# Building one-hot coefficient tables: second-key compares in bf16, cast to fp32 by ScalarE

## The chip, the core and the metric

The kernel runs on one core of a Trainium2 chip. The metric is the device time in microseconds of one execution, the median of several. The work is in fp32, with bf16 used for values that are exact in it (small whole numbers, zeros and ones).

## What is computed

One layer of a diffusion backbone over 128 context tokens and 512 latent tokens, width 1024: a projection, retention and neighbourhood attention, an output projection, and then a PEER layer, which is what matters here. Cut to that:

```python
def peer(x, wq, keys, u, v):          # 8 heads, product keys, 128 * 128 experts, top 16 per head
    q = (xb @ wq).reshape(TOKEN_BLOCK, PEER_HEADS, PEER_DKEY)
    s1 = jnp.einsum('nhd,hkd->nhk', q[..., :half], keys[:, 0])
    s2 = jnp.einsum('nhd,hkd->nhk', q[..., half:], keys[:, 1])
    ...
    eidx = jnp.take_along_axis(cidx, sel, axis=-1)        # i1 * 128 + i2
    gate = jax.nn.softmax(top, axis=-1)
    act = jax.nn.gelu(jnp.einsum('nd,nhkd->nhk', xb, u[eidx]))
    return jnp.einsum('nhk,nhkd->nd', gate * act, v[eidx])
```

Each of the 640 tokens picks 128 experts; for each, a row of `u` is dotted with the token, and a row of `v` is added with the weight `gate * act`.

## The kernel before, in words

Tokens go in five blocks of 128: block 0 is the context, blocks 1 to 4 the latents.

**The `u` half.** For all five blocks the rows of `u` are fetched by indirect DMA, issued by GpSimd: one gather brings one row to each of 128 tokens (512 KB), 128 gathers per block, 640 in all. They land in a handful of buffers in the arena. VectorE takes each with one dot product (`scalar_tensor_tensor` over 128x1024 with an accumulator, `gathers`, L1438, L1488), which frees the buffer for the next gather. The finding of the experts (`topk`, L1349) is VectorE work as well, with some casts on ScalarE.

**The `v` half.** For block 4 it is done in the same way, with 128 more gathers. Blocks 0 to 3 do without gathers: the weights of 128 tokens are written out as a dense coefficient table of 128 x 128 experts per token, and all of `v` (64 MB) is streamed through TensorE against it. `Dense.product(0)` does blocks 0 and 1, `Dense.product(1)` blocks 2 and 3; each has 512 matmuls 128x512, four for each tile of `v` (two blocks by two halves). `v` is read by SyncE's queue into a ring of six buffers.

**The tables.** `Dense.build(b)` (L1571) makes the table of block b, `W[b % 2]`. Its start turns the expert numbers into two key tables (`keys[:, 0]` the first key, `keys[:, 1]` the second, in bf16, one column per token) and the weights into `cT`; there is one set of these (`tabs`), so one build follows the other. Then it goes over the 128 tokens in pairs. For a pair, VectorE compares the first keys with 0..127 into `eq` (bf16) and the second keys into `B_` (fp32); ScalarE multiplies `eq` with the weight of each token into `A_` (fp32), two instructions; TensorE multiplies `B_` with `A_`, one matmul 128x128 per token, into a PSUM bank. After two pairs ScalarE copies the bank of four tokens into the table. I call two pairs, with that copy, a group: 32 groups per build, 128 in all. `eq`, `A_` and `B_` have two buffers each. For blocks 0 and 1 the copy writes with a stride (the table lies expert by token), for blocks 2 and 3 it writes whole rows, into rows that `product(0)` has done with. So `build(0)` and `build(1)` come before `product(0)`, `build(2)` runs beside it, and `build(3)` lies round its end, before `product(1)` can use its second table. `build(0)` runs beside `key_scores` (L913), the last stage of the projections.

**The order.** Nothing is issued as it is written. `Plan` records every operation (L167), gives it a cost from its engine, size and types (`cost`, L192), and a list scheduler (`forward`, L293, `backward`, `order`, L223) sets the order on each engine; line L365 of the trace, where the order is emitted, is therefore the line of nearly all instructions. On an engine, instructions run in that order, and one that waits holds up all behind it.

Of the kernel before, what the change touches and what calls it, by code (L numbers as in the profile page):

```python
# [12 lines left out]
BF16 = mybir.dt.bfloat16  # L13
# [3 lines left out]
AF = mybir.ActivationFunctionType  # L17
OP = mybir.AluOpType
# [3 lines left out]
P = 128  # L22
# [346 lines left out]
def layer(ctx: ExitStack, tc: tile.TileContext, a: dict):  # L369
    nc = Plan(tc.nc)  # L370
# [9 lines left out]
    iota2 = st.tile([P, P, 2], BF16, name="iota2")  # L380
# [32 lines left out]
    def bank():  # L413
        return ps.alloc([512], lo=banks[0], hi=banks[1])
# [11 lines left out]
    def mm(out, lhsT, rhs, start, stop):  # L426
        nc.tensor.matmul(out, lhsT=lhsT, rhs=rhs, start=start, stop=stop)
        k, m = lhsT.shape[0], int(np.prod(lhsT.shape[1:]))
        n = int(np.prod(rhs.shape[1:]))
        up = lambda v: 32 if v <= 32 else 64 if v <= 64 else 128  # L430
        clk["PE"] += 4 * n / 2400.0 * up(k) / 128 * up(m) / 128

    def tr(out, in_):
        nc.tensor.transpose(out, in_, ident)
        clk["PE"] += 0.216
# [118 lines left out]
    oneh, eqs, tabs, scb, spare = [], [], [], [], []  # L554

    def reserve():

        all_ = ar.alloc([19, P], lo=0, hi=12 * 256 // UNIT).ap
        oneh[:] = [all_[:, 4 * i:4 * i + 4].rearrange("s (z n) i -> s z n i", z=2) for i in range(2)]
        eqs[:] = [all_[:, 8 + i].bitcast(BF16).rearrange("s (i n) -> s i n", n=2) for i in range(2)]  # L560
        tabs[:] = [all_[:, 12], all_[:, 13], all_[:, 14].bitcast(BF16).rearrange("s (z n) -> s z n", z=2)]
        scb[:] = [all_[:, 15:19]]
        spare[:] = [all_[:, 0:8].rearrange("s a b -> s (a b)")]
# [388 lines left out]
    def ctx_front():  # L952
# [123 lines left out]
        ada(2, 1)  # L1076
        make_gates(0, ("g2",))
        reserve()
        done.add("ctx")

# [484 lines left out]
    class Dense:  # L1565
# [5 lines left out]
        def build(self, b):  # L1571

            g, q = divmod(b, 2)
            if self.W[q] is None:
                self.W[q] = ar.alloc([P, P], top=True)
            Wn = self.W[q].ap
            if g == 0:
                Wn = Wn.rearrange("j i n -> j n i")
            while (b, 3) not in cready:
                yield "wait"  # L1580

            bt = bank()
            tr(bt.ap[:, 0:P], cw[b].rearrange("q h k -> q (h k)"))
            cT, ti, keys = tabs
            tii = ti.bitcast(I32)
            id_ = idx[b].rearrange("q h k -> q (h k)")
            for z, (op, s) in enumerate(((OP.arith_shift_right, 7), (OP.bitwise_and, 127))):
                nc.vector.tensor_single_scalar(tii, id_, s, op=op)
                nc.vector.tensor_scalar(ti, tii, 1.0, None, op0=OP.mult)
                tr(bt.ap[:, P * (z + 1):P * (z + 2)], ti)  # L1590
            nc.scalar.copy(cT, bt.ap[:, 0:P])
            nc.scalar.copy(keys, bt.ap[:, P:3 * P].rearrange("s (z n) -> s z n", z=2))
            ps.free(bt)
            full = None
            for m in range(P // 2):
                n0 = 2 * m
                while g == 1 and self.at < min(n0 + 4, P) and n0 % 4 == 0:
                    yield "at"
                eq, A_, B_ = eqs[m % 2], oneh[m % 2][:, 0], oneh[m % 2][:, 1]
                nc.vector.tensor_tensor(eq, iota2, keys[:, 0, None, n0:n0 + 2].to_broadcast([P, P, 2]), op=OP.is_equal)  # L1600
                nc.vector.tensor_tensor(B_, iota2.rearrange("s i n -> s n i"),
                                        keys[:, 1, n0:n0 + 2, None].to_broadcast([P, 2, P]), op=OP.is_equal)
                if n0 % 4 == 0:
                    bw = bank()
                for k in range(2):
                    nc.scalar.activation(A_[:, k], eq[:, :, k], AF.Copy, scale=cT[:, n0 + k:n0 + k + 1])
                if full is not None:
                    nc.scalar.copy(*full)
                    ps.free(last)
                    full = None  # L1610
                for k in range(2):
                    z = n0 % 4 + k
                    mm(bw.ap[:, P * z:P * z + P], B_[:, k], A_[:, k], True, True)
                if n0 % 4:
                    full, last = (Wn[:, n0 - 2:n0 + 2, :], bw.ap.rearrange("j (n i) -> j n i", n=4)), bw
                    yield
            nc.scalar.copy(*full)
            ps.free(last)
# [194 lines left out]
```

## Time and profile before

| | |
|---|---|
| median of three runs | 1906.23 us (1904.07 to 1906.36) |
| profiled execution | 1904.95 us, of which the span from first to last instruction is 1903.1 us |
| busy: PE | 1777.2 us (93%) |
| busy: DVE | 1467.7 us (77%) |
| busy: ACT | 532.2 us (28%) |
| busy: POOL | 834.4 us (44%) |
| mean granted TensorE clock | 0.958 |
| DMA | 658.22 MB, mean 346 GB/s |

PE is TensorE, PEld its loading of weights, DVE VectorE, ACT ScalarE, POOL GpSimd, SP SyncE. Shares are means over stages that have different limits. A record of a matmul 128x512 in fp32 comes twice per matmul. Records of instructions on one engine overlap at their ends, so that what one instruction costs its engine is read from start to start, not from its length.

### The profile page before, as it was taken

Reading aid. Unit: us, or ns where it says so; the run is one execution under the profiler, and the core shown is the slowest. Engines: PE = TensorE matmul, PEld = TensorE weight load, DVE = VectorE, ACT = ScalarE, POOL = GpSimd, SP = SyncE. Lnnn points to the kernel's source line nnn. Section 1 sums busy time; section 2 is a strip of 40 time slices with the busy share of each in tenths; the row PEclk is TensorE's granted clock in tenths of the full one; section 3 lists DMA queues with packets and bytes.
Section 4 is the critical chain, followed back from the end, with each engine's and each line's share of the span. In section 5 each row is a group of like instructions: output and inputs, shape, how many; then the busy total and the mean of one; then the engine's idle time right before and its main releaser. Section 6 shows DMA issues by size and latency. Waiting matters only on the chain.

```text
span 1903.1 us, 21175 instructions
## 1 busy us (share of the span) xinstructions
PE 1777.2 (93%) x6096; PEld 1063.2 (56%) x6096; DVE 1467.7 (77%) x3785; ACT 532.2 (28%) x1368; POOL 834.4 (44%) x779
## 2 busy tenths in 40 slices
PE   7999999999999889867999999899987999999997
PEld 2438454455965466555444444355665666666665
DVE  2246998786879999999999996777998566666666
ACT  1225320133434334698211110122674000000000
POOL 0000467542137666524555544444435344444442
PEclk9998999999979889977999999899997999999999
DMA  9997889988759999857999999999978999999998
GB/s 363 316 327 246 313 278 339 393 311 307 271 178 344 365 336 378 317 177 210 364 408 401 392 408 409 387 409 406 358 242 275 410 409 409 409 409 409 409 409 330
DMA packets 203693, 658.22 MB, mean 346 GB/s; under 512 B 22572, under 2 KB 25900, under 8 KB 203448
## 3 DMA queue, kind: packets, MB, share of 16 engines
q0 software_dynamic: 110592, 402.70, 56.7%
q1 hardware_dynamic: 92984, 254.16, 35.5%
q8 instruction: 49, 0.80, 0.2%
q14 instruction: 68, 0.56, 0.1%
HBM read 645.51 MB, written 11.27 MB: 345 GB/s over the span
## 4 chain that ended last, share of the span: by engine, by line
DMA 27%; DVE 18%; PE 12%; issue 6%; ACT 2%; POOL 1%; DVEq 0%; POOLq 0%; ACTq 0%
DMA arena<-in_u,idx 15%; PE psum L365 12%; DMA arena<-in_v,idx 12%; DVE arena L365 12%; ACT arena L365 2%; DVE psum L365 1%; POOL arena L365 1%; DVE i L365 1%; DVE oh L365 1%; DVE vi L365 1%; DVE cand L365 0%; DVE idx L365 0%; DVE pi L365 0%; DMA w<-xres 0%; DMA out_y<-w 0%
## 5 line engine op out<-in xcount | busy, mean ns | idle before, releaser
L365 PE MATMUL psum<-w,arena 128*128 128x512 f32 (+1 forms) x2548 | 1094.2, 600 | 17.4 <-DVE arena L365 6.5
L365 POOL DMA_INDIRECT arena<-in_u,idx x640 | 711.6, 1112 | 899.8 <-DVE arena L365 486.6
L365 PEld LDWEIGHTS psum<-w,arena 128*128 128x128 f32 (+1 forms) x2548 | 560.4, 229 | 456.3 <-issue 280.2
L365 PE MATMUL psum<-arena 128*128 128x128 f32 (+5 forms) x2532 | 543.4, 366 | 65.3 <-ACT arena L365 34.1
L365 PEld LDWEIGHTS psum<-arena 128*128 128x128 f32 (+2 forms) x2532 | 374.3, 206 | 273.8 <-issue 137.3
L365 DVE SCALAR_TENSOR_TENSOR arena<-arena 128x1024 f32<-128x1024 f32 (+5 forms) x451 | 488.7, 1091 | 27.6 <-DMA arena<-in_u,idx 25.0
L365 DVE SCALAR_TENSOR_TENSOR arena<-arena,psum 128x1024 f32<-128x1024 f32 x256 | 308.4, 1214 | 92.6 <-DMA arena<-in_u,idx 92.6
L365 ACT ACTIVATE arena<-arena 128x128 f32<-128x128 bf16 (+7 forms) x626 | 237.7, 433 | 224.4 <-PE psum L365 103.8
L365 ACT COPY arena<-psum 128x512 f32<-128x512 f32 (+3 forms) x360 | 204.0, 581 | 316.6 <-PE psum L365 287.0
L365 DVE SCALAR_TENSOR_TENSOR psum<-arena,cw,psum 128x1024 f32<-128x1024 f32 x127 | 163.7, 1289 | 96.1 <-DMA arena<-in_v,idx 96.0
L365 DVE TENSOR_TENSOR arena<-iota,arena 128x256 f32<-128x256 bf16 (+1 forms) x512 | 160.7, 355 | 36.1 <-PE psum L365 33.3
L365 POOL DMA_INDIRECT arena<-in_v,idx x128 | 119.9, 937 | 141.5 <-DVE psum L365 118.1
L365 PE MATMUL psum<-arena,w 128*128 128x128 f32 (+1 forms) x640 | 132.0, 365 | 1.6 <-ACT arena L365 1.6
L365 PEld LDWEIGHTS psum<-arena,w 128*128 128x128 f32 x640 | 92.9, 196 | 31.4 <-ACT arena L365 2.3
L365 PE MATMUL psum<-ident,arena 128*128 128x128 f32 x372 | 64.9, 302 | 30.6 <-DVE arena L365 28.1
L365 PEld LDWEIGHTS psum<-ident,arena 128*128 128x128 f32 x372 | 48.7, 157 | 66.2 <-DVE arena L365 32.4
L365 DVE TENSOR_TENSOR arena<-arena 128x256 f32<-128x256 f32 (+6 forms) x131 | 61.0, 497 | 6.6 <-ACT arena L365 3.7
L365 ACT ACTIVATE zz<-dots 128x64 f32<-128x64 f32 x10 | 2.6, 255 | 196.3 <-DVE arena L365 196.3
L365 DVE TENSOR_TENSOR arena<-psum,arena 128x512 f32<-128x512 f32 (+1 forms) x40 | 27.1, 688 | 35.8 <-PE psum L365 34.7
L365 DVE TENSOR_REDUCE arena<-arena 128x8 f32<-128x512 f32 (+1 forms) x17 | 12.6, 743 | 46.2 <-ACT arena L365 46.2
L365 ACT ACTIVATE arena<-psum,arena 128x128 f32<-128x128 f32 (+2 forms) x102 | 34.7, 429 | 31.8 <-PE psum L365 27.6
L365 DVE MAX8 vi<-arena 128x8 f32<-128x128 f32 x128 | 30.0, 279 | 11.0 <-ACT arena L365 11.0
(74 smaller groups left out, 498.8 us busy)
## 6 DMA issues: line engine op xcount, KB each, us to landing
w<-in_v SPq DMA_DIRECT2D x251, 512.0 KB, 6.8
w<-in_w_ada SPq DMA_DIRECT2D x41, 512.0 KB, 5.4
w<-in_wq SPq DMA_DIRECT2D x40, 512.0 KB, 5.7
w<-in_w_in SPq DMA_DIRECT2D x36, 512.0 KB, 10.3
arena<-in_u,idx POOLq DMA_INDIRECT x640, 8.0
arena<-in_w_in SPq DMA_DIRECT2D x16, 512.0 KB, 9.4
w<-in_w_out SPq DMA_DIRECT2D x16, 512.0 KB, 5.7
arena<-in_x SPq DMA_DIRECT2D x9, 512.0 KB, 6.8
```

The costliest lines, as they stand in the source:

```text
L365: getattr(getattr(self.nc, eng), fn)(*args, **kw)
```

## The change

All second keys are compared in bf16, together with the first: one VectorE instruction over 512 elements per pair takes the place of two over 256. `eq` becomes twice as large (it takes space that was free), and ScalarE gets one instruction more per pair, a cast of 256 elements from bf16 to fp32, which writes `B_`.

```diff
-        eqs[:] = [all_[:, 8 + i].bitcast(BF16).rearrange("s (i n) -> s i n", n=2) for i in range(2)]
+        eqs[:] = [all_[:, 8 + 2 * i:10 + 2 * i].rearrange("s a b -> s (a b)").bitcast(BF16)
+                  .rearrange("s (z i n) -> s z i n", z=2, n=2) for i in range(2)]
...
                 eq, A_, B_ = eqs[m % 2], oneh[m % 2][:, 0], oneh[m % 2][:, 1]
-                nc.vector.tensor_tensor(eq, iota2, keys[:, 0, None, n0:n0 + 2].to_broadcast([P, P, 2]), op=OP.is_equal)
-                nc.vector.tensor_tensor(B_, iota2.rearrange("s i n -> s n i"),
-                                        keys[:, 1, n0:n0 + 2, None].to_broadcast([P, 2, P]), op=OP.is_equal)
+                nc.vector.tensor_tensor(eq, iota2[:, None].to_broadcast([P, 2, P, 2]),
+                                        keys[:, :, None, n0:n0 + 2].to_broadcast([P, 2, P, 2]), op=OP.is_equal)
+                nc.scalar.copy(B_, eq[:, 1].rearrange("s i n -> s n i"))
...
                 for k in range(2):
-                    nc.scalar.activation(A_[:, k], eq[:, :, k], AF.Copy, scale=cT[:, n0 + k:n0 + k + 1])
+                    nc.scalar.activation(A_[:, k], eq[:, 0, :, k], AF.Copy, scale=cT[:, n0 + k:n0 + k + 1])
```

In all: 512 compares on VectorE become 256 of twice the size, and ScalarE gets 256 casts. The planner sees other costs and sets another order, in the whole program. Three things of it:

ScalarE in the middle of `build(1)`. Before, `ACTIVATE arena<-arena` are the multiplications into `A_`, and `COPY arena<-psum` is the copy of four tokens into the table:

```order
L365 ACTIVATE arena<-arena 128x128 x4
L365 COPY arena<-psum 128x4x128
L365 ACTIVATE arena<-arena 128x128 x4
L365 COPY arena<-psum 128x4x128
L365 ACTIVATE arena<-arena 128x128 x4
L365 COPY arena<-psum 128x4x128
```

Now, with `CAST arena<-arena 128x256` the new cast into `B_`:

```order
L365 CAST arena<-arena 128x256
L365 ACTIVATE arena<-arena 128x128 x2
L365 CAST arena<-arena 128x256
L365 ACTIVATE arena<-arena 128x128 x2
L365 COPY arena<-psum 128x4x128
L365 ACTIVATE arena<-arena 128x128
L365 CAST arena<-arena 128x256
L365 ACTIVATE arena<-arena 128x128
L365 COPY arena<-psum 128x4x128
```

A group has five instructions before and seven now.

VectorE in the middle of `build(1)`. Before, `TENSOR_TENSOR arena<-iota` are the compares (four a group) and `SCALAR_TENSOR_TENSOR` the dot products with gathered rows:

```order
L365 TENSOR_TENSOR arena<-iota_65,arena 128x256 x4
L365 SCALAR_TENSOR_TENSOR arena,dots_77<-arena 128x1024
L365 TENSOR_TENSOR arena<-iota_65,arena 128x256 x4
L365 SCALAR_TENSOR_TENSOR arena,dots_77<-arena 128x1024
L365 TENSOR_TENSOR arena<-iota_65,arena 128x256 x4
L365 SCALAR_TENSOR_TENSOR arena,dots_77<-arena 128x1024
```

Now (`MAX tv<-cand` and `MAX_INDEX pi` belong to the finding of experts):

```order
L365 TENSOR_TENSOR arena<-iota_65,arena 128x512
L365 MAX tv<-cand 128x8
L365 SCALAR_TENSOR_TENSOR arena,dots_77<-arena 128x1024
L365 TENSOR_TENSOR arena<-iota_65,arena 128x512 x2
L365 MAX tv<-cand 128x8
L365 SCALAR_TENSOR_TENSOR arena,dots_77<-arena 128x1024
L365 TENSOR_TENSOR arena<-iota_65,arena 128x512
L365 MAX_INDEX pi<-tv,cand 128x8
L365 SCALAR_TENSOR_TENSOR arena,dots_77<-arena 128x1024
```

More dot products, and some of the finding of experts, now stand between the compares of the same table. Counted through: before the first compare of `build(0)` stand 204 dot products (now 208), before the last of `build(1)` 303 (now 322), before the first of `build(2)` 444 (now 465), before the first of `build(3)` 525 (now 546), before its last 557 (now 588).

On TensorE the matmuls of the builds keep their places among those of the products: the first of `build(2)` stands behind 350 product matmuls (now 351), its last behind 500 (now 500), the first of `build(3)` behind 502 (now 502), its last behind 524 (now 524). On ScalarE, when the last scores of `key_scores` have been copied, 52 of the 256 multiplications of `build(0)` and `build(1)` stand in front of that copy, and now 42.

## Rows read from the trace of the kernel before

**Rows 1.** The windows view: microseconds, busy time by engine (instructions), clock, DMA, by stage

```profile
core 0: us, PE busy (x) PEld busy (x) DVE busy (x) ACT busy (x) POOL busy (x), PEclk, DMA share, GB/s
786.00:911.00 125.00, 89.78 (x436) 71.78 (x435) 119.49 (x338) 110.41 (x266) 47.26 (x48) 0.81 0.67 206
...
911.00:1205.00 294.00, 293.15 (x689) 129.46 (x688) 265.98 (x907) 37.48 (x109) 150.53 (x137) 1.00 1.02 401
1205.00:1217.00 12.00, 2.69 (x5) 0.95 (x4) 7.89 (x18) 0.54 (x2) 5.62 (x6) 0.63 1.03 409
1217.00:1376.00 159.00, 159.00 (x559) 86.29 (x558) 132.44 (x302) 59.90 (x170) 76.90 (x81) 1.00 1.00 389
...
1376.00:1460.00 84.00, 64.18 (x304) 48.49 (x303) 77.57 (x208) 57.70 (x161) 31.75 (x33) 0.84 0.77 249
1460.00:1891.00 431.00, 429.53 (x1006) 295.71 (x1006) 268.36 (x306) 3.81 (x12) 191.07 (x204) 1.00 1.02 405
```

**Rows 2.** The chain of waits, 1455 to the end: shares by line

```profile
by line: DMA arena<-in_v,idx 52.5%; DMA arena<-in_u,idx 31.5%; issue 5.4%; DVE psum L365 5.4%; DVE arena L365 2.7%; POOL arena L365 2.4%; DVE w L365 0.3%; DVEq L1805 0.1%; DVEq L365 0.1%; POOLq L1805 0.1%; POOLq L365 0.0%
```

**Rows 3.** Groups by form on ScalarE, 786 to 911: count, busy us, mean ns, idle before

```profile
L365 ACT ACTIVATE arena<-arena 128x128 f32<-128x128 bf16 x204 | 66.0, 395 | 7.0 <-DVE arena L365 4.1 <-PE psum L365 2.8
L365 ACT COPY arena<-psum 128x512 f32<-128x512 f32 x53 | 54.0, 1030 | 7.6 <-PE psum L365 7.3
```

**Rows 4.** ScalarE's timeline late in `build(1)`: start us, us, instructions, count

```profile
884.90 1.26 ACT L365 ACTIVATE arena<-arena 128x128 f32<-128x128 bf16 x4
886.16 1.04 ACT L365 COPY arena<-psum 128x512 f32<-128x512 f32 x1
887.00 1.26 ACT L365 ACTIVATE arena<-arena 128x128 f32<-128x128 bf16 x4
888.26 1.05 ACT L365 COPY arena<-psum 128x512 f32<-128x512 f32 x1
889.09 1.26 ACT L365 ACTIVATE arena<-arena 128x128 f32<-128x128 bf16 x4
```

**Rows 5.** Groups by form, whole run: the nearest rows to the new instructions

```profile
L365 ACT CAST arena<-psum 128x256 bf16<-128x256 f32 x4 | 1.5, 373 | 78.6 <-PE psum L365 78.6
L365 ACT COPY arena<-psum 128x384 f32<-128x384 f32 x16 | 7.4, 476 | 27.0 <-PE psum L365 27.0
L365 DVE TENSOR_TENSOR oh<-oh,cidx 128x800 int16<-128x800 bf16 x40 | 22.6, 565 | 0.0
L365 DVE TENSOR_TENSOR oh<-oh,i 128x1600 bf16<-128x1600 bf16 x20 | 19.7, 984 | 3.6 <-ACT oh L365 3.6
L365 DVE TENSOR_TENSOR arena<-iota,arena 128x256 f32<-128x256 bf16 x256 | 105.6, 419 | 34.3 <-PE psum L365 33.3
L365 DVE TENSOR_TENSOR arena<-iota,arena 128x256 bf16<-128x256 bf16 x256 | 70.5, 291 | 1.8 <-ACT arena L365 1.4
```

**Rows 6.** VectorE's timeline in `build(3)`: start us, us, instructions, count

```profile
1426.73 1.21 DVE L365 TENSOR_TENSOR arena<-iota,arena 128x256 bf16<-128x256 bf16 x4
1427.86 1.21 DVE L365 SCALAR_TENSOR_TENSOR arena<-arena,psum 128x1024 f32<-128x1024 f32 x1
1429.00 0.08 DVE L365 DVE_READ_ACCUMULATOR arena<-arena,psum 128x1 f32 x1
1429.00 0.41 DVE L365 TENSOR_TENSOR w<-psum,w 128x256 f32<-128x256 f32 x1
1429.34 1.21 DVE L365 TENSOR_TENSOR arena<-iota,arena 128x256 bf16<-128x256 bf16 x4
```

**Rows 7.** Groups by form, 1376 to 1460 (first row), 1461 to 1511 (second)

```profile
L365 ACT COPY arena<-psum 128x512 f32<-128x512 f32 x31 | 17.8, 576 | 7.4 <-PE psum L365 7.3
...
L365 DVE SCALAR_TENSOR_TENSOR arena<-arena,psum 128x1024 f32<-128x1024 f32 x25 | 29.8, 1215 | 19.1 <-DMA arena<-in_u,idx 19.1
```

**Rows 8.** TensorE's timeline before `build(2)`: its wait for the key tables

```profile
1215.04 0.48 PE L365 MATMUL psum<-ident,arena 128*128 128x128 f32 x1 [9.31 <-DVE arena L365]
```

## The prediction

> **What bounds the kernel now.** I read the program by stages first, then who waits in each. From 786 us, when the last key scores are copied, to 911 us only the first two tables are built, beside dot products [rows 1]: PE is busy for 89.8 of 125 us at a granted clock of 0.81, the DMA engines are used to 0.67, VectorE is busy for 119.5 us and ScalarE for 110.4 us. So the stage belongs to these two. From 911 us the first product runs, and PE has no hole: 293.15 of 294 us, then 159.00 of 159 us with the third table's matmuls in between; the only break is 1205 to 1217 us [rows 1], where PE waits 9.31 us for the third table's keys behind dot products on VectorE [rows 8]. From 1376 to 1460 us the fourth table is built (84 us, VectorE busy for 77.6). The second product then takes PE 429.5 of 431 us [rows 1]. In that last stage the chain of waits names gathers instead [rows 2]: they fill the DMA queues (share 1.02). PE and gathers end together; neither has time to spare.
>
> It follows that the time is made of two starts. If the first product starts later, PE is late by as much until 1376 us, for it is full all the way. If the fourth table is done later, the second product starts later, and the end moves by as much.
>
> **What the change takes off VectorE.** In the steady stretch [rows 6], four compares hold it from 1426.73 to 1427.86 us: 1.13 us. An fp32 instruction over 256 elements holds it for 0.34 us (1429.00 to 1429.34), so the two in fp32 make 0.68 us, and those in bf16 0.22 us each. The new instruction is not in the trace; between 800 and 1600 elements bf16 costs 0.52 ns more per element (565 and 984 ns [rows 5]), so 512 elements come to 0.415 us as a record, and without the overlap of 0.07 us that the record of 256 elements has (291 ns [rows 5] against 0.22 us), to 0.345 us. Two of them make 0.69 us instead of 1.13 us: 0.44 us less per group, 56 us over 128 groups. VectorE also loses its wait for PE to release `B_`, 33.3 us in the whole run [rows 5]: the cast on ScalarE takes that wait over.
>
> **What it puts on ScalarE.** Late in the second table ScalarE is already full: multiplications start at 884.90, 887.00 and 889.09 us, with no idle time between, so a group costs it 2.10 us [rows 4]. A cast of 256 elements from bf16 to fp32 inside SBUF has no row. Nearest below: casts of 256 elements from PSUM, 373 ns [rows 5], less the overlap of 0.105 us that ScalarE's records have (four multiplications of 395 ns [rows 3] end 1.26 us after the first starts [rows 4], so they stand 0.29 us apart): 0.27 us. Nearest above: a multiplication, 0.29 us, with 128 elements more at 0.78 ns (384 elements take 476 ns [rows 5], 512 take 576 ns [rows 7]): 0.39 us, although this has a weight per partition to read. I take 0.31 us, near the row with the same size. Two per group make 0.62 us, and a group 2.72 us.
>
> Here a page speaks against the change more strongly than I do. The Trainium skill, "VectorE: DVE Perf Modes", section on the TRN2 errata, gives a ScalarE instruction inside SBUF 224 cycles and one per element at 1.2 GHz, so 400 ns for this cast (an estimate); by it the first product would start 10 us later than in my sum. "ScalarE: Activation LUTs", section on what ACT_TABLE_LOAD costs, has 186 ns and 0.833 ns per element for an instruction without pointer operands, and 93 ns of overlap between neighbours: 306 ns, an estimate that would leave my sum as it is. No run here shows yet which of them holds for a cast between neighbours.
>
> **The first start.** From the last key scores on, ScalarE had 204 multiplications left, which is 51 groups [rows 3]; in the new order it has 214, 53.5 groups. Before: 51 x 2.10 = 107 us of the 125; the rest is 14.6 us idle [rows 1] and a few small instructions (about 4 us). Now: 53.5 x 2.72 = 145.5, with 4 for the small ones 149.5 us, and between none and all of the 14.6 us of waits. I take half, since the copy of four tokens now has part of the next group in front of it, in which PE can finish: 157 us, or 32 us more than before. VectorE can't be what ends this stage later than that: its compares shrink, and the planner has filled the room with dot products (322 instead of 303 before the last compare). Nothing covers the 32 us: PE has only the first table, and of `v` the six buffers.
>
> **The second start.** The matmuls of builds and products stand in the same places on PE, so the fourth table begins 32 us later too, unless the 9.31 us hole [rows 8] closes; by the counts of dot products it does not (below), so I count nothing for it. The build itself: VectorE has 42 dot products at 1.14 us (start to start [rows 6]), 64 compares at 0.345 and 16 additions of the finish at 0.34 us: 75 us. ScalarE has 32 groups; here the copy writes whole rows and takes 576 ns [rows 7], 0.47 without the overlap, so 4 x 0.29 + 0.47 + 0.62 = 2.25 us a group, 72 us. With VectorE's 6.4 us of idle time as before (84 - 77.6): 81 us instead of 84. Together 32 - 3 = 29 us.
>
> **Sum.** 1904.95 us of the profiled execution (span 1903.1), plus 29: **1934 us**. This execution lies 1.3 us under the median of the runs, which changes nothing. Low end of this case: casts of 0.27 us (-4), no waits (-7), the hole closed (-9): 1914. High end: casts of 0.39 us (+9), all waits (+7), the build no shorter (+3): 1953.
>
> **Are the gathers there in time?** The last compare of the fourth table now stands behind 588 dot products instead of 557. Before, 25 came in the 50 us after 1461 [rows 7], so number 588 fell at about 1522 us, 33 us after the 1489 us that I need. Three things bring it forward. At 943 us, 322 are done; before, 141 came between 911 and 1217 us (303 to 444), so 322 fell at 952: 9 us ahead. The stream of `v` starts 32 us later, which leaves its share of the DMA to gathers: 512 KB per four matmuls of 0.855 us (1006 records, two per matmul, in 429.53 us [rows 1]), 5 MB, 9 gathers, some 20 us. And from 1376 to 1460 us the DMA had moved 249 GB/s where it moves 405 elsewhere [rows 1], as VectorE was at the compares. So they are just in time, and the hole of 9.31 us stays.
>
> **Rivals.** *VectorE is the bound of the builds, and the kernel gets faster.* For it: VectorE is busy for 119.5 of 125 us, ScalarE for 110.4 [rows 1]. If ScalarE could take the casts into its idle time, 51 groups would lose 0.44 us each (22 us), and the fourth table 3 us: 1880 us. Against: 14.6 us of idle time over 107 casts is 0.14 us a cast; the lowest bound is 0.27, and rows 4 show groups without any idle time. The point from which it decides is a group of 2.45 us (125/51) or less on ScalarE. 0.13.
>
> *The delay is hidden.* Between 1376 and 1460 us PE is idle for 20 us of 84 [rows 1]. If the fourth table were built while the first product still runs, its late end would cost nothing: 1905 us. Against: it needs rows that the product frees, and stands behind 502 product matmuls as before. 0.07.
>
> *Gathers starve.* A compare that waits for ScalarE to read `eq` holds up the dot products behind it, and GpSimd's queue waits for their buffers. If the stream of gathers gains nothing over before, dot product 588 falls at 1522 us, and the end moves by 62: 1967 us. It decides if number 588 comes after 1489. For it: the order counts on 31 more; against: the three points above. 0.12.
>
> **Numbers.** My forecast has 0.68. 1934 is its time. The range takes in the hidden delay below and half of the starving above: 1905 to 1960; left out are the faster rival and the upper part of the last, under 0.2. Two runs of this kernel can be told apart by about 0.2%. Faster 0.13, same 0.07, slower 0.68 + 0.12 = 0.80.
>
> **What would show it.** In the profile after: casts `arena<-arena` of 256 elements, 256 of them, 0.37 to 0.5 us as records; compares of 512 elements near 415 ns; ScalarE's busy time up by about 100 us, VectorE's down by about 70; the two first tables done at about 943 us, with ScalarE busy for over 95% from the last key scores on; PE full from there; the last compare at about 1490 us and the second product 431 us long behind it. I am wrong if the first product starts before 925 us, if ScalarE has idle time in this stage while VectorE has none, or if the second product starts where it did.

## The result, and the profile after

The changed kernel takes **1926.5 us** (median of four runs, 1923.88 to 1933.05) against 1905.15 us for the kernel before, measured beside it (four runs, 1894.42 to 1906.36). The ratio is 1.0134, with an interval of 1.0104 to 1.0165: **slower**, as forecast, by 21 us instead of 29. The profiled execution took 1926.19 us, its span is 1924.4 us.

The windows view of the kernel after, cut at the same events as [rows 1] (us, busy time by engine with instructions, clock, DMA share, GB/s):

```profile
core 0: us, PE busy (x) PEld busy (x) DVE busy (x) ACT busy (x) POOL busy (x), PEclk, DMA share, GB/s
794.00:941.00 147.00, 109.35 (x458) 88.09 (x458) 135.83 (x343) 145.90 (x398) 66.16 (x67) 0.68 0.73 240
941.00:1234.00 293.00, 291.59 (x684) 129.03 (x683) 252.40 (x808) 33.22 (x93) 144.45 (x138) 1.00 1.02 406
1234.00:1246.00 12.00, 5.21 (x13) 1.96 (x11) 8.05 (x17) 0.99 (x4) 5.79 (x7) 0.85 1.01 401
1246.00:1404.00 158.00, 157.69 (x553) 86.29 (x554) 117.49 (x233) 77.02 (x230) 76.40 (x82) 0.99 1.00 390
1404.00:1488.00 84.00, 69.33 (x306) 51.44 (x305) 77.23 (x165) 74.72 (x226) 39.35 (x42) 0.84 0.89 307
1488.00:1919.00 431.00, 429.91 (x1003) 295.55 (x1004) 234.08 (x251) 2.97 (x9) 161.08 (x172) 1.00 0.94 368
```

The first stage has grown from 125 to 147 us, and ScalarE is busy for 145.90 of them, where it was busy for 110.41 of 125. From there the program runs as before: 293 us of product, a hole of PE, 158 us with the third table, 84 us for the fourth, 431 us of product.

What fills ScalarE is seen in its groups by form, 794 to 941 us (count, busy us, mean ns, idle before):

```profile
L365 ACT ACTIVATE arena<-arena 128x128 f32<-128x128 bf16 x214 | 82.6, 435 | 0.4 <-DVE w L365 0.4
L365 ACT COPY arena<-psum 128x512 f32<-128x512 f32 x55 | 57.0, 1055 | 0.0
L365 ACT CAST arena<-arena 128x256 f32<-128x256 bf16 x107 | 46.7, 437 | 0.2 <-PE psum L365 0.2
```

Against [rows 3] the idle time before multiplications and copies is gone (7.0 and 7.6 us, now 0.4 and 0.0). What a cast costs is read from start to start in ScalarE's timeline (start us, us, instructions, count):

```profile
898.35 0.43 ACT L365 ACTIVATE arena<-arena 128x128 f32<-128x128 bf16 x1
898.64 0.43 ACT L365 CAST arena<-arena 128x256 f32<-128x256 bf16 x1
898.93 0.44 ACT L365 ACTIVATE arena<-arena 128x128 f32<-128x128 bf16 x1
899.24 1.05 ACT L365 COPY arena<-psum 128x512 f32<-128x512 f32 x1
900.04 0.44 ACT L365 ACTIVATE arena<-arena 128x128 f32<-128x128 bf16 x1
900.33 0.44 ACT L365 CAST arena<-arena 128x256 f32<-128x256 bf16 x1
900.63 0.74 ACT L365 ACTIVATE arena<-arena 128x128 f32<-128x128 bf16 x2
```

The cast holds ScalarE for 0.29 us (898.64 to 898.93) or 0.30 us (900.33 to 900.63). The new pair over the whole run, by form, answers to [rows 5]:

```profile
L365 DVE TENSOR_TENSOR arena<-iota,arena 128x512 bf16<-128x512 bf16 x256 | 105.9, 425 | 52.9 <-ACT arena L365 51.1
L365 ACT CAST arena<-arena 128x256 f32<-128x256 bf16 x256 | 105.4, 412 | 26.4 <-DVE arena L365 25.6 <-PE psum L365 0.6
```

VectorE's wait for PE (33.3 us) has become a wait for ScalarE (51.1 us). Of the chain of waits from 1480 us to the end, the shares by line and its last two long pieces (start us, us, what):

```profile
by line: DMA arena<-in_v,idx 49.7%; DMA arena<-in_u,idx 17.8%; PE psum L365 14.8%; DVE psum L365 5.1%; DVE arena L365 3.7%; issue 3.2%; DMA w<-in_v 1.9%; POOL arena L365 1.3%; DMA w<-g2d 0.7%; DVE w L365 0.6%; DVE zz L365 0.2%; SPq L365 0.1
...
1847.18 65.69 PE psum L365 x152
...
1912.89 3.31 DMA w<-g2d
```

In [rows 2] gathers carried the chain to the end. Now it is PE's from 1847 us on: the product alone ends the program.

**Where the 21 us are.** Four events of the trace cut each profiled span into four parts: the last copy of key scores into `w` on ScalarE (786 us in [rows 1]; two more copies of scores, which go into the arena, follow within 5 us in the kernel before, so that the stage is not quite free of `key_scores`), the start of the last multiplication of `build(1)`, that of `build(3)`, and the end. *Dots* are the dot products that VectorE starts in the second part, and in the time of `build(3)`, whose length (first to last multiplication) stands beside it. The experiments ran on three more chips: e1 to e4 on one, r1, r2, e6 and e7 on the next, e5, e8, e9 and r3 on the third. So each ratio, of medians, is to the kernel before on the same chip. The other columns are of one profiled execution each, and only the first chip and that of r2_before_again have a trace of the kernel before; for the other two chips the parts are compared with r2_before_again, which leaves their fronts without a measure.

| kernel | front | stage | middle | rest | span | dots in stage | build(3) us, dots | ratio to before |
|---|---|---|---|---|---|---|---|---|
| before | 785.8 | 125.2 | 549.0 | 443.1 | 1903.1 | 47 | 83.1, 32 | |
| change | 793.7 | 147.1 | 546.9 | 436.7 | 1924.4 | 68 | 83.3, 43 | 1.0134 |
| r2_before_again | 802.4 | 124.3 | 547.8 | 442.6 | 1917.1 | 47 | 82.0, 32 | |
| r1_change_again | 807.5 | 148.7 | 546.6 | 435.6 | 1938.4 | 68 | 83.1, 43 | 1.0089 |
| e6_idle_cast | 798.0 | 148.5 | 540.2 | 443.8 | 1930.5 | 53 | 76.4, 30 | 1.0093 |
| e7_no_cast | 809.1 | 114.1 | 534.7 | 437.9 | 1895.8 | 50 | 70.3, 33 | 0.9849 |
| e1_late | 806.9 | 124.0 | 548.7 | 436.3 | 1915.9 | 44 | 82.7, 46 | 1.0031 |
| e2_early | 798.4 | 145.8 | 538.4 | 440.0 | 1922.6 | 71 | 75.0, 27 | 0.9992 |
| e3_after_copy | 808.2 | 137.5 | 545.8 | 436.4 | 1927.9 | 68 | 83.5, 43 | 1.0002 |
| e4_before_copy | 799.6 | 120.2 | 548.9 | 443.1 | 1911.8 | 47 | 81.6, 32 | 0.9945 |
| e8_half | 805.4 | 128.3 | 543.3 | 441.4 | 1918.4 | 51 | 78.2, 30 | 0.9953 |
| e9_half_copy | 801.6 | 115.6 | 541.5 | 439.0 | 1897.7 | 51 | 76.4, 30 | 0.9875 |
| e5_dve_cast | 795.3 | 121.3 | 545.9 | 443.6 | 1906.1 | 47 | 77.7, 28 | 0.9937 |
| r3_before_copy_again | 796.5 | 118.1 | 547.7 | 442.0 | 1904.3 | 47 | 81.3, 32 | 0.9950 |

In the first two rows the difference of 21.3 us is 7.9 in the front, 21.9 in the stage, -2.1 in the middle and -6.4 in the rest.

### The profile page after: what moved, and what is told of

Read it like the earlier page. It is cut to its first block, busy times and chain, and to the rows that moved or that the text cites. A ratio compares the mean times of both kernels' runs of the same rounds, so it can differ in the third digit from the quotient of the medians.

```text
span 1924.4 us, 20753 instructions
## 1 busy us (share of the span) xinstructions
PE 1802.0 (94%) x6096; PEld 1081.2 (56%) x6096; DVE 1414.8 (74%) x3529; ACT 601.3 (31%) x1624; POOL 815.8 (42%) x779
## 4 chain that ended last, share of the span: by engine, by line
DMA 29%; DVE 15%; PE 15%; ACT 5%; issue 4%; POOL 1%; SPq 0%; DVEq 0%; ACTq 0%; POOLq 0%
DMA arena<-in_u,idx 16%; PE psum L365 15%; DMA arena<-in_v,idx 11%; DVE arena L365 10%; ACT arena L365 5%; DVE psum L365 1%; DVE i L365 1%; DMA w<-in_v 1%; DVE oh L365 1%; POOL arena L365 1%; DVE vi L365 1%; DMA w<-xres 1%; DMA out_y<-w 1%; DVE w L365 0%; DVE cand L365 0%
## 5 line engine op out<-in xcount | busy, mean ns | idle before, releaser
L365 POOL DMA_INDIRECT arena<-in_u,idx x640 | 693.0, 1083 | 878.3 <-DVE arena L365 445.4
L365 PE MATMUL psum<-arena 128*128 128x128 f32 (+5 forms) x2532 | 565.1, 377 | 75.1 <-ACT arena L365 64.2
L365 PEld LDWEIGHTS psum<-arena 128*128 128x128 f32 (+2 forms) x2532 | 388.8, 212 | 291.1 <-issue 135.7
L365 DVE SCALAR_TENSOR_TENSOR arena<-arena 128x1024 f32<-128x1024 f32 (+6 forms) x451 | 489.0, 1093 | 35.7 <-DMA arena<-in_u,idx 34.2
L365 ACT ACTIVATE arena<-arena 128x128 f32<-128x128 bf16 (+7 forms) x626 | 261.6, 448 | 201.2 <-PE psum L365 89.8
L365 DVE TENSOR_TENSOR arena<-iota,arena 128x512 bf16<-128x512 bf16 x256 | 105.9, 425 | 52.9 <-ACT arena L365 51.1
L365 ACT CAST arena<-arena 128x256 f32<-128x256 bf16 x256 | 105.4, 412 | 26.4 <-DVE arena L365 25.6
L365 DVE TENSOR_TENSOR arena<-psum,arena 128x512 f32<-128x512 f32 (+1 forms) x40 | 27.1, 685 | 33.3 <-PE psum L365 32.9
## 6 DMA issues: line engine op xcount, KB each, us to landing
arena<-in_w_in SPq DMA_DIRECT2D x16, 512.0 KB, 10.8
```

Of the source, the lines that this page charges most:

```text
L365: getattr(getattr(self.nc, eng), fn)(*args, **kw)
```

## The experiments

Two theories stood against each other. **S**: ScalarE is full in the stage, so each cast there delays the first product and with it the end. **Its rival** (theory O in the expectations of e1 to e4): the joint compare and the new order on VectorE (more dot products between compares, a longer way from compare to matmul) cost the time, whichever engine casts.

**r1_change_again and r2_before_again** have no edit: both kernels once more, with profiles of the same chip.

> The changed kernel once more, beside the kernel before on the same chip. The loss has four parts in the first pair of traces: the last key scores are copied 8 us later, the stage from there to the first product alone is 22 us longer, from there to the second product it is 4 us shorter, and the tail after the last matmul is 6 us shorter. Theory S: the 22 us stay on any chip, and the time is 12 to 24 us above before. Theory F (a good part of the loss is the front, where the granted clock falls for a while between 500 and 575 us, by chance or by chip): the loss shrinks to 5 to 15 us where before falls too.

> The kernel before with a profile of this chip. Stage from the last key scores to the first product alone: 124 to 127 us, as in the first trace; the last key scores: theory F has them later than 786 us by 5 to 20 us, with the clock low for longer between 500 and 575 us.

Measured: 1938.32 us (six runs) against 1921.35 (eleven), ratio 1.0089 (1.0060 to 1.0118). The spans differ by 21.3 us again: 5.1 in the front, 24.4 in the stage, -1.2 and -7.0. Stage, middle and rest of each kernel repeat within 2 us on another chip; the fronts are 14 to 17 us longer there. So a stage that is longer by 22 to 24 us belongs to the change.

**e6_idle_cast** is the kernel before, with one ScalarE cast per pair more, whose result nobody reads:

```diff
+                nc.scalar.copy(idle[0], eq.rearrange("s i n -> s n i"))
                 if n0 % 4 == 0:
                     bw = bank()
```

> The kernel before, and on ScalarE one cast per pair of the first compare into a buffer that nobody reads; VectorE's work stays as it was. Theory S: the stage from the last key scores takes 145 to 155 us as with the change, since ScalarE's load alone sets it, and the time is 20 to 35 us above before (the gathers do not run ahead, so the tail does not shrink). If the loss came from VectorE's new instruction or from ScalarE as a new link between compare and matmul, this kernel would lose under 10 us.

Measured: 1938.97 us (four runs), ratio 1.0093 (1.0071 to 1.0114), as much as the change itself on the same chip. Its stage in the windows view, and its ScalarE there, by form:

```profile
798.00:946.00 148.00, 116.30 (x463) 91.01 (x462) 133.51 (x378) 143.60 (x379) 59.75 (x59) 0.65 0.71 212
```

```profile
L365 ACT ACTIVATE arena<-arena 128x128 f32<-128x128 bf16 x213 | 84.1, 467 | 2.4 <-PE psum L365 2.1 <-remote 0.3
L365 ACT COPY arena<-psum 128x512 f32<-128x512 f32 x55 | 58.8, 1090 | 0.0
L365 ACT CAST arena<-arena 128x256 f32<-128x256 bf16 x106 | 49.9, 470 | 2.0 <-DVE arena L365 1.2 <-issue 0.6
```

VectorE still has the 512 old compares here, and only 53 dot products in the stage instead of the change's 68. The stage is 148.5 us all the same, with ScalarE busy for 97% of it and VectorE for 90%. That speaks for S: casts on ScalarE are enough for a loss as large as the change's, without the joint compare and without 15 of the dot products. The time is 17.6 us over the kernel before, where 20 to 35 was expected; 7.6 us come back in the middle (`build(3)` takes 76.4 us instead of 82.0).

**e7_no_cast** has the joint compare and no cast; TensorE multiplies `A_` with `A_`, so the second keys are left out of the tables:

```diff
-                nc.scalar.copy(B_, eq[:, 1].rearrange("s i n -> s n i"))
...
-                    mm(bw.ap[:, P * z:P * z + P], B_[:, k], A_[:, k], True, True)
+                    mm(bw.ap[:, P * z:P * z + P], A_[:, k], A_[:, k], True, True)
```

> The new joint compare, but no cast: the tables are the product of A_ with itself, so the second key does not reach them and the outputs of blocks 0 to 3 lack their experts. This shows what VectorE's relief is worth alone. Theory S: ScalarE has 2.10 us a group as before and VectorE 0.4 us less, so the stage from the last key scores shrinks to 108 to 118 us, and the time is 10 to 25 us below before. If VectorE's time did not matter, it would be the time of before.

Measured: 1894.72 us (four runs), ratio 0.9849 (0.9825 to 0.9874). The windows view of its stage:

```profile
809.00:924.00 115.00, 83.37 (x442) 68.61 (x441) 103.42 (x238) 107.72 (x263) 52.45 (x55) 0.90 0.78 252
```

Without casts the joint compare is a gain of 27 us (10 to 25 was expected): 10 in the stage and 13 in the middle, where `build(3)` falls to 70.3 us. So VectorE, by its work and its wait for `B_`, did hold up the kernel before in both places. The two effects don't add: an idle cast alone costs 18 us, but on top of the joint compare casts cost 44 us (1938.32 - 1894.72). Two things differ between these two kernels, and e7_no_cast does not part them: ScalarE's load, and the planner's order, which has 68 dot products in the change's stage and 50 here.

**e1_late and e2_early** put the new form in blocks 2 and 3 only, or in blocks 0 and 1 only:

```diff
+                if g == 1:
                     nc.vector.tensor_tensor(eq, iota2[:, None].to_broadcast([P, 2, P, 2]),
...
+                else:
+                    nc.vector.tensor_tensor(eq[:, 0], iota2, keys[:, 0, None, n0:n0 + 2].to_broadcast([P, P, 2]), op=OP.is_equal)
```

(`g == 0` in e2_early.)

> The new compare and cast in blocks 2 and 3 alone, the old two compares in blocks 0 and 1. Theory S (ScalarE is full while the first two tables are built, and the later first product is all of the loss): the first product runs alone from 905 to 920 us as before, the fourth table takes 81 to 84 us, the time is 1898 to 1910 us. Theory O (the new order that the planner makes from new costs is the loss, the casts are not): the order is new here too, and the time stays 10 us or more above before, 1915 to 1930 us.

> The new compare and cast in blocks 0 and 1 alone. Theory S: the first product starts at 935 to 945 us with ScalarE busy for over 97% of the stage before, and the time is 1922 to 1936 us, all of the loss. If half of the loss came from blocks 2 and 3, it would be 1912 to 1918 us. Theory O: anywhere between before and after.

Measured: e1_late 1928.64 us (ten runs) against 1923.35 (31 runs), ratio 1.0031 (1.0012 to 1.0050); e2_early 1920.14 us (ten runs), 0.9992 (0.9975 to 1.0008). The stage does what S says: 124.0 us with the old form there, 145.8 with the new. The totals do not: by S e1_late was to lie between 7 us under and 5 over the kernel before (it is 5.3 over), and e2_early was to have all of the loss. e2_early gets some 12 of its 21 us back in the middle and the rest: the 24 dot products that VectorE did early are missing later, `build(3)` has 27 instead of 32 and takes 75.0 us with the old compares, and the gathers end sooner. Where the other 9 go is not shown, for this chip has no trace of the kernel before. So the delay of the first product is not always passed on whole. e1_late gains nothing from cheaper compares in `build(3)`, because the planner put 46 dot products there instead of 32. Why it is 0.3% slower than before stays open: its profiled execution (1917.65 us) was the fastest of its ten runs, and does not show it.

**e3_after_copy and e4_before_copy** make ScalarE's copy into the tables of blocks 0 and 1 cheaper, in the change and in the kernel before. The copy went token by token, each word 512 bytes from the last; now it goes expert by expert and writes four neighbouring words:

```diff
-                    full, last = (Wn[:, n0 - 2:n0 + 2, :], bw.ap.rearrange("j (n i) -> j n i", n=4)), bw
+                    dst, src = Wn[:, n0 - 2:n0 + 2, :], bw.ap.rearrange("j (n i) -> j n i", n=4)
+                    if g == 0:
+                        dst, src = (x.rearrange("j n i -> j i n") for x in (dst, src))
+                    full, last = (dst, src), bw
```

> The changed kernel, but the copy of four tokens into the first two tables goes expert by expert, so that it writes four neighbours at a time instead of one value every 512 bytes. If the copy then takes its 0.57 us of the later tables instead of 1.05, theory S has 53.5 groups of 2.35 instead of 2.72 us: the first product starts 15 to 20 us earlier than with the change, and the time is 1906 to 1913 us. If reading PSUM with a stride is as slow as the writing was, nothing changes (1924 to 1930 us). Theory O: no change from the copy's length, since the planner does not see it: 1926 us in either case.

> The kernel before with that copy alone. Theory S: ScalarE was busy for 110 of 125 us there and VectorE for 119, so a shorter copy frees ScalarE but VectorE's compares and dot products stay: the first product starts 0 to 8 us earlier, the time is 1897 to 1906 us.

> The kernel before with the new copy, again, beside the other three: 0.992 to 0.997 over before, the stage 120 us. If e9_half_copy is under it, joint compares help where ScalarE has room for half of the casts; if not, they give nothing even there.

Measured: e3_after_copy 1923.66 us (ten runs), ratio 1.0002 (0.9985 to 1.0019); e4_before_copy 1912.85 us (ten runs), 0.9945 (0.9925 to 0.9964); again on a further chip 1911.77 us (six runs), 0.9950 (0.9931 to 0.9970). The copy's row in e3_after_copy's stage (by form), and that stage in the windows view:

```profile
L365 ACT COPY arena<-psum 128x512 f32<-128x512 f32 x56 | 31.4, 567 | 0.0
```

```profile
808.00:947.00 139.00, 105.51 (x461) 82.39 (x461) 134.36 (x351) 131.50 (x402) 77.68 (x68) 0.80 0.78 268
```

The copy's record is 567 ns instead of 1055; from start to start it holds ScalarE for 0.47 us instead of 0.83 (medians of the two stages). With time taken off ScalarE alone, the change loses nothing any more against the kernel before; that is S again. But the stage shrinks by 10 us, not by the 20 that 55 copies save: VectorE, with 68 dot products, is now busy for 134.36 of 139 us. Its joint compares in the stage, first in the change and then in e3_after_copy (by form):

```profile
L365 DVE TENSOR_TENSOR arena<-iota,arena 128x512 bf16<-128x512 bf16 x106 | 44.0, 428 | 10.3 <-ACT arena L365 8.7
```

```profile
L365 DVE TENSOR_TENSOR arena<-iota,arena 128x512 bf16<-128x512 bf16 x106 | 42.2, 416 | 0.7 <-ACT arena L365 0.5
```

The compares no longer wait for ScalarE, so it is VectorE that sets these 137.5 us. In the kernel before VectorE is the next limit sooner, with 47 dot products; the stage of e4_before_copy:

```profile
800.00:920.00 120.00, 87.86 (x437) 70.97 (x436) 117.85 (x338) 95.96 (x266) 48.23 (x48) 0.82 0.71 215
```

There the copy brings 4 to 6 us in the stage, of 10 to 11 in all; where the others come from is not shown. And there is something in the rival: with the same copy and on the same chip, the change is still 10.8 us slower than the kernel before (1923.66 against 1912.85). What is left when ScalarE has room goes with the order that puts 21 more dot products into the stage.

**e8_half and e9_half_copy** share the load: the first pair of a group has the new form, the second the old one; e9_half_copy has the new copy too.

```diff
+                if n0 % 4 == 0:
                     nc.vector.tensor_tensor(eq, iota2[:, None].to_broadcast([P, 2, P, 2]),
...
+                else:
+                    nc.vector.tensor_tensor(eq[:, 0], iota2, keys[:, 0, None, n0:n0 + 2].to_broadcast([P, P, 2]), op=OP.is_equal)
```

> Only the first pair of every group has the new form (joint compare, cast on ScalarE), the second pair the old one. Theory 'ScalarE is full in the stage': a group costs it 2.10 + 0.30 = 2.40 us, 52 to 53 groups 125 to 127 us, so from the last key scores to the first product 127 to 132 us (before 125, change 148), ScalarE busy for over 93% of it; time over before 1.000 to 1.006. Rival 'VectorE is the bound wherever ScalarE has a little room, and the planner's extra dot products set its work': the stage is as long as VectorE's work, 117 to 124 us, with VectorE busy for over 96%; 0.994 to 0.999.

> The half form, and the copy into the tables of blocks 0 and 1 writes runs of four words (1.05 to 0.57 us each). ScalarE's group then costs 1.92 us, 101 us in all, so by the theory ScalarE no longer bounds the stage and VectorE does: 112 to 120 us (before 125), VectorE busy for over 95%; time over before 0.990 to 0.996, at or under the kernel before with the new copy alone (0.9945). If the planner fills all the room with dot products: 120 to 126 us and 0.996 to 1.000.

Measured: e8_half 1915.14 us (seven runs) against 1922.89 (twelve), ratio 0.9953 (0.9934 to 0.9972); e9_half_copy 1899.11 us (five runs), 0.9875 (0.9857 to 0.9894). Their stages:

```profile
805.00:934.00 129.00, 95.80 (x444) 76.15 (x443) 115.75 (x299) 124.17 (x320) 56.57 (x55) 0.79 0.75 233
```

```profile
802.00:918.00 116.00, 85.60 (x431) 68.10 (x432) 112.65 (x293) 107.62 (x318) 53.64 (x54) 0.87 0.80 256
```

In e8_half ScalarE is busy for 96% of 129 us, which is what S expected of the stage; the total was to be 0 to 0.6% longer and is 0.5% shorter. About 4 us of that are in `build(3)` (78.2 us); the remainder can't be read from the profile, whose execution (1920.17 us) was the slowest of the seven. In e9_half_copy VectorE is busy for 97%; the stage is as expected, and the time better than the 0.990 to 0.996. Both engines now take the same time for a group, as the timelines show, VectorE's first and ScalarE's second (rows of the same group and the start of the next; the three compares of a group, one joint and two old, stand merged under the form of the first):

```profile
882.88 1.00 DVE L365 TENSOR_TENSOR arena<-iota,arena 128x512 bf16<-128x512 bf16 x3
883.81 1.21 DVE L365 SCALAR_TENSOR_TENSOR arena<-arena 128x1024 f32<-128x1024 f32 x1
...
884.95 1.00 DVE L365 TENSOR_TENSOR arena<-iota,arena 128x512 bf16<-128x512 bf16 x3
```

```profile
882.86 0.56 ACT L365 COPY arena<-psum 128x512 f32<-128x512 f32 x1
883.39 0.40 ACT L365 ACTIVATE arena<-arena 128x128 f32<-128x128 bf16 x1
883.70 0.40 ACT L365 CAST arena<-arena 128x256 f32<-128x256 bf16 x1
884.01 1.01 ACT L365 ACTIVATE arena<-arena 128x128 f32<-128x128 bf16 x3
884.93 0.56 ACT L365 COPY arena<-psum 128x512 f32<-128x512 f32 x1
```

2.07 us on either (882.88 to 884.95, 882.86 to 884.93). This is the fastest of the kernels here that compute the whole layer: 1.25% under the kernel before, and 0.7% under the kernel before with the new copy alone, beside it on the same chip (1899.11 against 1911.77).

**e5_dve_cast** has the change's joint compare, with the cast on VectorE:

```diff
-                nc.scalar.copy(B_, eq[:, 1].rearrange("s i n -> s n i"))
+                nc.vector.tensor_copy(B_, eq[:, 1].rearrange("s i n -> s n i"))
```

> The change with the cast on VectorE in place of ScalarE. Theory 'what costs is ScalarE's time': ScalarE's group is 2.10 us again; VectorE's compares and casts of a group make 2 x 0.345 + 2 c with c from 0.22 to 0.34 us, so 1.13 to 1.37 us against 1.13 before: the stage is 125 to 137 us, over before 1.000 to 1.010. Rival 'the order of the joint compare costs, whichever engine casts' (dot products between, the longer chain compare, cast, matmul): 145 us or more, 1.009 or more.

Measured: 1908.81 us (six runs), ratio 0.9937 (0.9916 to 0.9957), better than either theory. VectorE's timeline in its `build(1)`:

```profile
871.02 0.28 DVE L365 CAST arena<-arena 128x256 f32<-128x256 bf16 x1
871.23 0.75 DVE L365 TENSOR_TENSOR arena<-iota,arena 128x512 bf16<-128x512 bf16 x2
871.90 0.28 DVE L365 CAST arena<-arena 128x256 f32<-128x256 bf16 x1
872.10 1.21 DVE L365 SCALAR_TENSOR_TENSOR arena<-arena 128x1024 f32<-128x1024 f32 x1
```

The cast holds VectorE for 0.20 us (871.90 to 872.10), a joint compare for 0.335 us. A group makes 1.08 to 1.13 us of VectorE's time, no more than the 1.13 before, and ScalarE's load is back to what it was, as the stage shows:

```profile
795.00:918.00 123.00, 88.14 (x438) 73.35 (x437) 120.78 (x333) 113.86 (x271) 47.26 (x47) 0.79 0.69 211
```

The same compare and the same cast, on the other engine, turn a loss into a gain: what costs is not the joint compare, nor the longer way from compare to matmul. The rival's other half, the 68 dot products, is not tested here, since the planner put 47 into this stage, as before; e3_after_copy beside e4_before_copy is what speaks on it. Of the gain of 14 us the traces place 3 in the stage and 2 in the middle, where `build(3)` has 28 dot products instead of 32; where the others come from is not shown.

## Why the prediction was right, and where it was off

**The sign and the mechanism held.** "ScalarE is already full" late in the second table, and the stage passes its delay on: PE runs without a hole from the first product to the third table, and the second product takes 431 us as before. (With another order behind it, in e2_early, some 12 of 21 us come back.) That the first two tables end at 941 us, where 943 was forecast, is luck: the front is 8 us longer than before and the stage 10 us shorter than in the sum. And "VectorE can't be what ends this stage later than that" holds by only 10 us: where ScalarE has room, VectorE's 68 dot products hold the stage at 137.5 us (e3_after_copy).

**The cast.** Predicted 0.31 us, measured 0.29 to 0.30. Of the two figures weighed there, the one of the Trainium skill, "ScalarE: Activation LUTs", section on what ACT_TABLE_LOAD costs, agrees with this (306 ns, an estimate from it). The 400 ns estimated from the Trainium skill, "VectorE: DVE Perf Modes", section on the TRN2 errata, is near the length of the cast's record (412 ns in the mean), and not what a cast between neighbours costs in this trace.

**The first start: 157 us predicted, 147 measured.** Most of the miss is "I take half" of the 14.6 us of waits: the groups of ScalarE show 0.6 us of idle time, the window 1.1 us. That makes 6 of the 10 us. The rest is the group: 2.72 us predicted; 145.9 us less 4 for small instructions, over 53.5 groups, is 2.65 us, and 53.5 x 0.07 is 4 us. Both lie between what I took and my low end.

**The second start: right by luck.** `build(3)` was to take 81 instead of 84 us, and the hole of [rows 8] was to stay. The middle did shrink, by 2.1 us, but the other way round. From first to last compare `build(3)` takes 82.7 instead of 84.2 us, but from first to last multiplication 83.3 instead of 83.1 (83.1 instead of 82.0 on r2_before_again's chip). The hole is 7.10 us instead of 9.31 (7.2 instead of 9.0 there), with another owner. TensorE's timeline:

```profile
1246.31 1.01 PE L365 MATMUL psum<-arena 128*128 128x128 f32 x3 [7.10 <-ACT arena L365]
```

VectorE's gain of 14 us (0.44 us times 32 groups) went into 11 more dot products (43 instead of 32, 12.5 us), as the prediction had counted (42). The 75 us of VectorE's work were too low by 2: it is busy for 77.23 of 84 us, as it was before. e7_no_cast, with 33 dot products and no casts, takes 70.3 us.

**The gathers were in time, and the end is the step that failed.** Number 322 was to be done at 943 us and starts at 937.6; number 588 was wanted by 1489 us and starts at 1485.5. The dot products of `build(3)` hardly wait for gathers (VectorE by form, 1404 to 1488 us):

```profile
L365 DVE SCALAR_TENSOR_TENSOR arena<-arena,psum 128x1024 f32<-128x1024 f32 x43 | 52.0, 1208 | 0.3 <-DMA arena<-in_u,idx 0.3
```

But "PE and gathers end together; neither has time to spare" was true of the kernel before and not of the change. The last addition of a gathered row starts at 1849 us, before at 1891, while PE ends at 1920 us, before at 1892. So PE ends the program alone: what comes after its last matmul takes 4.7 us instead of 11.0, and the rest shrinks by 6.4 us. The sum had nothing for this: a lead of some 40 us of the gathers is worth 6.

**The front** was not in the sum, and is 7.9 us longer (5.1 on the other chip). In e6_idle_cast, which has the casts, it is 4.4 us shorter than in the kernel before on the same chip, and in e7_no_cast, which has none, 6.7 us longer: casts beside `key_scores` do not explain it. Nor does any other new instruction: the first of them, the first compare of `build(0)`, already starts 8.5 us later than before (695.4 against 686.9 us; 711.2 against 701.7 on the other chip). VectorE's order differs from the kernel before from about 185 us on; whether that is the cause stays open.

So 32 - 3 = 29 us was forecast, and 21.9 - 2.1 + 7.9 - 6.4 = 21.3 us came. The two terms that were left out nearly cancel, which is luck; the stage, 10 us shorter than in the sum, makes most of the difference. **Busy times**: ScalarE's was to rise by 100 us and rose by 69 (532.2 to 601.3), VectorE's was to fall by 70 and fell by 53 (1467.7 to 1414.8). I added lengths of records there; where neighbours overlap, busy time counts the overlap once. The rival "VectorE is the bound" was wrong about the change, and right about what the kernel before could gain: e7_no_cast gives 27 us.

## What to carry to other kernels

When work moves from one engine to another, add up a repeating group on both, from start to start: here 2.27 us on VectorE with one dot product (1.13 + 1.14) and 2.10 on ScalarE left room for 0.17 us where the casts took 0.6; half of the casts and a cheaper copy made both 2.07. Look also at what a scheduler puts into the room that a change makes: dot products of a stream that is not late used up VectorE's gain in the fourth table, and in the stage they would have been the next limit. Before an instruction is given to another engine because that engine is less busy in the mean, try it on the engine that the work comes from: the cast was 0.20 us there against 0.30.

## What the runs showed of the hardware that I had not expected

- ScalarE's copy of 128x512 fp32 from PSUM has records of 1055 ns with each written word 512 bytes from the last (the change; 1030 ns in [rows 3]), and of 567 ns with runs of four words, reading PSUM in another order (e3_after_copy). 571 ns in e9_half_copy agrees.
- ScalarE's records of the same multiplication differ in length from trace to trace (395 ns in [rows 3], 435 ns after, 467 ns in e6_idle_cast), though starts stay 0.29 to 0.30 us apart. The record's length is not the price. What lengthens it is not shown: it is 398 ns in e3_after_copy, where ScalarE is busy for 131.50 of 139 us.
- The same kernel differs by chip: the kernel before has medians of 1905.15 us on the first chip and 1921.35 to 1923.35 us on the others. In the two traces of it, which have the same instructions in the same order on VectorE, ScalarE and GpSimd, the difference lies in the front. From 525 to 575 us the first chip and then r2_before_again's show (windows):

```profile
525.00:550.00 25.00, 24.40 (x94) 18.11 (x92) 19.67 (x50) 9.71 (x23) 5.05 (x5) 0.59 0.44 141
550.00:575.00 25.00, 24.97 (x121) 14.60 (x120) 20.86 (x59) 10.22 (x32) 14.76 (x12) 1.00 0.72 231
```

```profile
525.00:550.00 25.00, 25.00 (x96) 20.47 (x95) 16.18 (x40) 5.69 (x14) 5.48 (x5) 0.50 0.28 84
550.00:575.00 25.00, 24.97 (x94) 15.79 (x94) 17.89 (x45) 9.96 (x29) 7.37 (x7) 0.76 0.41 118
```

The granted clock of TensorE stays at its lower level (0.50 is 1.2 of 2.4 GHz) for longer there, with PE busy all the time and 84 instead of 141 GB/s on the DMA. The front is 16.6 us longer, and some 14 of these arise between dot products number 120 and 140 (452 to 565 us on the first chip). Which comes first, the clock or the slower DMA, no run here tells; there is one trace of this kernel on either chip.
